# First pair of FFN up projections by eight plain products, token sums formed beside it, second norm at highest priority

## The chip, the cores and the metric

One core of a Trainium2 chip runs the whole program. The metric is the device time of one execution in microseconds (us), taken as the median of several runs. Engines are named as in the profile: PE is TensorE, DVE is VectorE, ACT is ScalarE, POOL is GpSimd, and SP is the queue from which most transfers are issued.

## What is computed

The reference is a two-layer trunk (a gated DeltaNet layer, then a retention layer). Each layer has a token mixer and a SwiGLU FFN. The change lies in the up projections of the first layer's FFN:

```python
x = x + gt1 * y                                   # end of the mixer
h = modulate(x, norm2_g[i], sh2, sc2)             # RMSNorm, scale, shift
x = x + gt2 * ((silu(h @ w1) * (h @ w3)) @ w2)    # the same for the context tokens
```

There are 512 latent and 256 context tokens, 1024 channels, and an FFN width of 2816, which is 22 tiles of 128 columns. All of it is in float32.

## The kernel before

A float32 operand is split into a high part that PE takes (fp32r) and a low remainder: ACT writes the high part (L113), DVE the low one (L114). A product is then three matmuls: high by high, low by high, high by low (`mm3`). The 768 tokens are joined in one tile `xj` (8 channel tiles by 768 tokens) and cut into two halves of 384, U1 and U2.

**The up projections** (`up_pairs`) take the 22 column tiles as 11 pairs. For one pair the work is a 2 by 2 block product: two column tiles, two halves of the channels, two halves of the tokens. Instead of eight block products the kernel forms seven, after Strassen and Winograd. The token blocks are `b11`, `b21` (U1, first and second channel half) and `b12`, `b22` (U2); the sums of them that the seven products need are `t1` to `t4`, made in `token_sums` on DVE (L447) with their high parts on ACT (L450). The weight sums `s1`, `s2` and two differences are made on POOL (L134). One block product is 24 matmuls of 128x384 (both of w1 and w3, four channel tiles, three matmuls each), so a pair is 168 matmuls.

**The first norm** (U1) is finished while the mixer's output projection still runs. Then `up_pairs` begins. Its first block product (`b11` by tile 0) needs only U1; `first` makes it and copies it to `p1`, and `second` adds the `b21` product and gates it. **The second norm** (U2) is a chain: POOL's last additions into `accj` (squares), the column sums on PE (`rstd_cols`, L315), about a dozen small operations on DVE (`rsqrt`, L169 to L176), three `diag` tiles spread by PE (L329), eight multiplications on DVE (L433), eight scalings on ACT (L440). Only then can `token_sums` begin, and five of the seven products of every pair need what it makes (`t1` to `t4`) or `b22` (`rest`). The kernel before opens pairs 0 and 1 (`first`, `second` of each), and after the token sums ends both with `rest`.

**The order** on each engine is made by the tile scheduler, which takes instructions by the place where they are written, or earlier where `high_priority()` stands around them; each engine then runs its instructions strictly in that order. DVE work marked with `keep_in_program_order` stays in the written order. The banks `psg` are three, and the converted weights are kept in rings of pools `wra`, `wrb` of two each. A raw weight tile is 1 MB, loaded by `up_load` from the SP queue: even tiles to pool `r8a`, odd ones to `r8b` and `r8c`. `xj` is given back after the token sums (`xjes.close()`); the pools opened behind it take its place. From pair 2 on `ada_rows` runs beside the products: every 10 groups of three matmuls it puts one load and one DVE reduction (L216 `prod`) into the stream, for the modulation of the next layer.

Of the kernel before, what the change touches and what calls it, by code (L numbers as in the profile page):

```python
# [10 lines left out]
F32 = mybir.dt.float32  # L11
# [18 lines left out]
J = 2  # L30
HALF = NT // 2
# [23 lines left out]
class Trunk:  # L55
# [370 lines left out]
    def norm_half(self, unit, r):  # L426
# [4 lines left out]
        for k in range(KT):  # L431
            x = self.xj[:, k, a:b]
            nc.vector.tensor_tensor(out=x, in0=x, in1=rb, op=ALU.mult)  # L433
            for st, lo, hi in PIECES[unit]:
# [4 lines left out]
                else:  # L439
                    nc.scalar.activation(out=v, in_=v, func=AF.Identity, scale=sc, bias=sh)  # L440

    def token_sums(self, pool):

        x, nc = self.xpart, self.nc

        def tt(o, a, b, op=ALU.subtract):
            self.tc.keep_in_program_order(nc.vector.tensor_tensor(out=o, in0=a, in1=b, op=op))  # L447

        at = lambda n, q, c: self.blocks[n][c][:, 2 * q:2 * q + 2, :]
        high = lambda n, q, src: nc.scalar.activation(out=at(n, q, 0), in_=src, func=AF.Copy)  # L450
        low = lambda n, q, src: tt(at(n, q, 1), src, at(n, q, 0).bitcast(F32))
        b11, b21, b12, b22 = ([x(h, u, q) for q in range(2)] for h in range(2) for u in range(2))
        for q in range(2):
            t3 = pool.tile([128, 2, HALF], F32, tag="t3", name="t3")
            tt(t3, b22[q], b12[q])
            tt(b11[q], t3, b11[q], ALU.add)
            high("t2", q, b11[q])
            high("t3", q, t3)
            tt(b21[q], b21[q], t3)
            low("t2", q, b11[q])  # L460
            low("t3", q, t3)
        for q in range(2):
            tt(b12[q], b22[q], b11[q])
            high("t1", q, b12[q])
        for q in range(2):
            low("t1", q, b12[q])
            high("t4", q, b21[q])
        for q in range(2):
            low("t4", q, b21[q])
            high("22", q, b22[q])  # L470
        for q in range(2):
            low("22", q, b22[q])

    def up_open(self, es):

# [11 lines left out]
        return new("") if kind == "s" else (new("h"), new("l"))  # L487

    def up_load(self, f):
        self.raws[f] = (self.ups["r"][0] if f % 2 == 0 else self.ups["r"][1:][f // 2 % len(self.ups["r"][1:])]).tile([128, 2, 1024], F32, tag="r", name="raw")  # L490
        self.nc.sync.dma_start(out=self.raws[f], in_=self.a["w13"][0, f].rearrange("j p c -> p j c"))

    def up_conv(self, src):
# [12 lines left out]
    def up_pairs(self, es, held):  # L506
# [3 lines left out]
        tt = nc.vector.tensor_tensor  # L510
        add, sub = ALU.add, ALU.subtract
        raws, blocks, conv = self.raws, self.blocks, self.up_conv
        self.block(self.pool(es, "late"), "t2", "t3", "t1", "t4", "22")
        pp = self.pool(es, "p1", 2)
        self.ups["w"].append(self.pool(es, "wrb", 2))
        self.ups["r"].append(self.pool(es, "r8c"))
        self.up_load(3)

        def product(ps, w, name, more=False):
            bh, bl = blocks[name]  # L520
# [18 lines left out]
        def first(w):  # L539
            a = bank()  # L540
            product(a, w, "11")
            p1 = pp.tile([128, 2, HALF], F32, name="p1")
            nc.scalar.activation(out=p1, in_=two(a), func=AF.Copy)
            return a, p1

        def second(i, a, w):
            product(a, w, "21", True)
            gate(a[:, 0, 0:HALF], a[:, 1, 0:HALF], 2 * i, U1)
# [25 lines left out]
            tt(out=u2, in0=two(c), in1=u2, op=add)  # L574
            gate(u2[:, 0, :], u2[:, 1, :], 2 * i, U2)

        a0, p0 = first(held["w"][0])
        w = conv(left(1)), conv(right(1))
        r = self.rstd_cols(U2, self.acc[J][:, U2[1]:U2[2]])
        a1, p1 = first(w[0])  # L580
        for q in range(2):
            tt(out=self.xpart(0, 1, q), in0=self.xpart(0, 1, q), in1=self.xpart(0, 0, q), op=sub)
        w2 = conv(held["sums"][1])
        self.norm_half(U2, r)
        second(0, a0, held["w"][1])
        second(1, a1, w[1])
        with ExitStack() as ts:
            self.token_sums(self.pool(ts, "tt"))
        self.xjes.close()
        begun = (a0, p0), (a1, p1)  # L590
        self.ups["s"].append(self.pool(es, "sb", 2))
        up = self.pool(es, "upk")
        ar = self.pool(es, "ar")
        for i in range(PAIRS):
            if i == 2:
                self.side, self.every = self.ada_rows(ar, ADA[0]), 10
            if i > 1:
                self.up_load(2 * i)
            if i > 1:
                self.up_load(2 * i + 1)  # L600
            if i < 2:
                rest(i, *begun[i], *((held["sums"], w2) if i == 0 else ()))
            else:
                a, p1 = first(conv(left(i)))
                rest(i, a, p1, mid=lambda: second(i, a, conv(right(i))))

    def down_groups(self, es, after):
        nc = self.nc
# [215 lines left out]
    def conv(self, pb, t):  # L824
        nc, cw = self.nc, self.cw
        cb = self.new([128, 770], "cb")
        nc.scalar.activation(out=cb, in_=pb[:, 0:770], func=AF.Copy, scale=cw[:, t, 0:1])  # L827
        for j in range(1, 5):
            last = nc.vector.scalar_tensor_tensor(out=cb, in0=pb[:, j:j + 770], scalar=cw[:, t, j:j + 1], in1=cb,  # L829
                                                  op0=ALU.mult, op1=ALU.add)  # L830
        return cb, last.ins
# [367 lines left out]
    def gdn(self):  # L1199
        nc, tc = self.nc, self.tc  # L1200
        with ExitStack() as es:
# [132 lines left out]
            for u in (U1, U2):  # L1334
                for m in range(KT):
# [14 lines left out]
                            for q in range(2):  # L1350
                                self.keep(name, q, self.xpart(0, up, q))
                    self.add_j(u, m, ps)
            held["sums"] = self.up_sums(0)
        return held

    def add_j(self, unit, m, ps):
# [301 lines left out]
```

## Time and profile before

| | |
|---|---|
| median of 3 runs | 2234.32 us (2232.72 to 2236.94) |
| profiled execution, own time | 2232.13 us |
| span of it in the trace | 2229.1 us |
| busy: PE, DVE, ACT, POOL | 2115.5, 1433.2, 835.5, 272.7 us |
| mean granted TensorE clock | 0.982 of full |

The profile page gives busy time per engine, the span in 40 slices, the chain of work that ended last, and the costliest groups of instructions. The trace answers narrower questions: a table of busy times by stretch (with the TensorE clock that was granted, as a share of full), a timeline by engine (start, duration, line, output and inputs, and in square brackets the idle time before it and what ended it), and the list of waits. A timeline row with "x2" stands for two instructions in a row. In the chain of waits 62% of the span is PE's products at L129.

### The profile page before, as it was taken

The numbers are of one execution on the slowest core, as the hardware profiler recorded it, in microseconds if no ns is written. First come the engines' busy times: TensorE is split into PE (matmuls) and PEld (weight loads), VectorE is DVE, ScalarE is ACT, GpSimd is POOL, SyncE is SP. The second block draws the span as 40 slices with busy tenths as digits, with TensorE's granted clock in tenths as the row PEclk, the third lists the DMA queues.
The fourth block names the chain that finished last, engine by engine and source line by source line (L and its number), as shares of the span: only waits on it lengthen the run. The fifth ranks groups of instructions, "written<-read, shape, count | busy, mean of one in ns | idle before, by whom it ended". The sixth has DMA issues, their size and how long they took to land.

```text
span 2229.1 us, 34569 instructions
## 1 busy us (share of the span) xinstructions
PE 2115.5 (95%) x13974; PEld 1825.6 (82%) x13974; DVE 1433.2 (64%) x2800; ACT 835.5 (37%) x1462; POOL 272.7 (12%) x218
## 2 busy tenths in 40 slices
PE   5899999999999779999999999999999999999997
PEld 2777887788767779999999988888888888888887
DVE  5786778677845768989766774645544466433435
ACT  3655656565623443333231242322222235222222
POOL 1322102221100533433100000000000000000000
PEclk9999999999999889999999999999999999999999
DMA  6221111111255333444475630312212123323221
GB/s 240 69 57 40 41 48 49 36 40 50 79 200 165 122 104 118 148 152 151 137 259 193 203 128 19 112 54 81 85 52 81 34 69 102 114 85 95 92 71 64
DMA packets 112384, 225.08 MB, mean 101 GB/s; under 512 B 47008, under 2 KB 60320, under 8 KB 111968
## 3 DMA queue, kind: packets, MB, share of 16 engines
q1 hardware_dynamic: 101264, 193.46, 26.7%
q10 hardware_dynamic: 8784, 23.07, 3.2%
q0 software_dynamic: 2176, 6.34, 0.9%
q8 instruction: 109, 1.79, 0.3%
q14 instruction: 51, 0.42, 0.1%
HBM read 203.84 MB, written 19.01 MB: 100 GB/s over the span
## 4 chain that ended last, share of the span: by engine, by line
PE 76%; DVE 10%; DMA 4%; ACT 4%; issue 3%; POOL 1%; SPq 0%; DVEq 0%; ACTq 0%; POOLq 0%
PE psg L129 62%; PE psx L129 13%; DVE wl L114 1%; DMA raw<-ada_t 1%; DVE cb L829 1%; PE psx L137 1%; DVE prod L216 1%; ACT wh L113 1%; DVE rsq_y L176 1%; DVE raw L216 1%; DMA graw<-gd 1%; ACT vd L1002 0%; DVE rsq_b L174 0%; DVE rsq_b L175 0%; DMA raw<-w 0%
## 5 line engine op out<-in xcount | busy, mean ns | idle before, releaser
L129 PE MATMUL psg<-hh,wh 128*128 128x512 f32 (+1 forms) x1152 | 426.3, 370 | 7.9 <-ACT pb L820 6.8
L129 PE MATMUL psg<-hl,wh 128*128 128x512 f32 (+1 forms) x1152 | 420.2, 365 | 2.0 <-POOL hl L284 1.7
L129 PE MATMUL psg<-hh,wl 128*128 128x512 f32 (+1 forms) x1152 | 418.9, 364 | 0.0
L113 ACT ACTIVATE wh<-raw 128x1024 fp32r<-128x1024 f32 (+1 forms) x203 | 209.0, 1030 | 553.9 <-PE psg L129 419.8
L114 DVE TENSOR_TENSOR wl<-raw,wh 128x1024 fp32r<-128x1024 f32 (+1 forms) x203 | 252.1, 1242 | 103.2 <-ACT wh L113 99.6
L129 PEld LDWEIGHTS psg<-hh,wh 128*128 128x128 f32 x1152 | 217.4, 189 | 38.8 <-ACT pb L820 8.0
L129 PEld LDWEIGHTS psg<-hl,wh 128*128 128x128 f32 x1152 | 217.6, 189 | 32.6 <-POOL hl L284 2.1
L129 PEld LDWEIGHTS psg<-hh,wl 128*128 128x128 f32 x1152 | 217.4, 189 | 30.3 <-DVE wl L114 0.2
L129 PE MATMUL psg<-gl,w2h 128*128 128x384 f32 (+2 forms) x560 | 193.4, 346 | 2.8 <-DVE gl L114 2.8
L129 PE MATMUL psg<-gh,w2h 128*128 128x384 f32 (+2 forms) x560 | 191.2, 346 | 4.4 <-ACT w2h L113 4.1
L129 PE MATMUL psg<-gh,w2l 128*128 128x384 f32 (+2 forms) x560 | 192.7, 345 | 0.4 <-DVE w2l L114 0.4
L354 DVE SCALAR_TENSOR_TENSOR x<-psg,mod,x 128x256 f32<-128x256 f32 (+3 forms) x192 | 105.1, 569 | 104.2 <-PE psg L129 103.7
L129 PEld LDWEIGHTS psg<-gh,w2h 128*128 128x128 f32 x560 | 105.8, 189 | 11.6 <-ACT w2h L113 4.4
L129 PEld LDWEIGHTS psg<-gl,w2h 128*128 128x128 f32 x560 | 106.3, 190 | 10.2 <-DVE gl L114 4.5
L129 PEld LDWEIGHTS psg<-gh,w2l 128*128 128x128 f32 x560 | 106.4, 190 | 6.5 <-DVE w2l L114 1.0
L829 DVE SCALAR_TENSOR_TENSOR cb<-pb,k_conv_w,cb 128x770 f32<-128x770 f32 x96 | 103.6, 1079 | 7.0 <-ACT cb L827 5.6
L216 DVE CUSTOM_DVE_ANT_0 raw<-raw,crow,k_ada_b 128x1024 f32<-128x1024 f32 x54 | 78.4, 1452 | 35.2 <-DMA raw<-ada_t 33.4
L113 ACT ACTIVATE w2h<-raw 128x1024 fp32r<-128x1024 f32 x48 | 50.5, 1056 | 113.8 <-PE psg L129 61.2
L129 PE MATMUL psg<-y,wh 128*128 128x512 f32 (+1 forms) x320 | 83.2, 350 | 0.0
L129 PE MATMUL psg<-wl,hh 128*128 128x512 f32 x192 | 75.0, 391 | 0.8 <-DVE wl L114 0.8
L129 PE MATMUL psg<-wh,hh 128*128 128x512 f32 x192 | 74.9, 390 | 0.0
L129 PE MATMUL psg<-wh,hl 128*128 128x512 f32 x192 | 74.9, 390 | 0.0
(406 smaller groups left out, 4451.5 us busy)
## 6 DMA issues: line engine op xcount, KB each, us to landing
raw<-w SPq DMA_DIRECT2D x88, 512.0 KB, 4.1
raw<-w_ret SPq DMA_DIRECT2D x64, 512.0 KB, 3.5
raw<-ada_t SPq DMA_DIRECT2D x54, 512.0 KB, 3.5
raw<-w SPq DMA_DIRECT2D x22, 1024.0 KB, 5.4
raw<-ada_w SPq DMA_DIRECT2D x42, 512.0 KB, 4.9
raw<-w_gdn ACTq DMA_DIRECT2D x31, 512.0 KB, 3.5
gd<-g SPq DMA_DIRECT2D x44, 192.0 KB, 1.8
graw<-gd SPq DMA_DIRECT2D x22, 384.0 KB, 4.7
```

Of the source, the lines that this page charges most:

```text
L113: nc.scalar.activation(out=hi, in_=src, func=AF.Copy)
L114: nc.vector.tensor_tensor(out=lo, in0=src, in1=hi.bitcast(F32), op=ALU.subtract)
L129: ins = self.nc.tensor.matmul(*args, **kw)
L137: ins = self.nc.tensor.transpose(out, in_, ident)
L176: nc.vector.scalar_tensor_tensor(out=y, in0=b, scalar=1.5, in1=y, op0=ALU.add, op1=ALU.mult)
L216: nc.vector.tensor_tensor_reduce(out=out, in0=raw, in1=cb[:, v, :], scale=1.0, scalar=self.adab[:, layer, col:col + 1], op0=ALU.mult, op1= ...
L354: self.nc.vector.scalar_tensor_tensor(out=x, in0=ps, scalar=self.mod[layer][:, 24 * which + 16 + m, 1 - st:2 - st], in1=x if src is None e ...
L829: last = nc.vector.scalar_tensor_tensor(out=cb, in0=pb[:, j:j + 770], scalar=cw[:, t, j:j + 1], in1=cb, op0=ALU.mult, op1=ALU.add)
```

## The change

Pair 0 (column tiles 0 and 1) is now formed by the plain eight products: `b11` and `b21` for both tiles, then, as soon as the second norm is ready, `b12` and `b22` for both. `b12` becomes a kept block of its own. Pair 1 is opened between the two (`first`, `second`). Its `rest`, and pairs 2 to 10, go on with seven products. The token sums, the weight sums of pair 1 and the splitting of `t1`, `t4` stand beside the eight products. The column sums, the whole second norm and the splitting of `b12` and `b22` stand in `high_priority()`. Tile 3 is loaded into the place of tile 1, a third ring of weights `wrc` is open meanwhile, and POOL's sums for pair 0 go.

```diff
+    def keep_block(self, name, src):
+        for q in range(2):
+            self.keep(name, q, src[q])
...
     def token_sums(self, pool):
...
         for q in range(2):
             tt(b12[q], b22[q], b11[q])
-            high("t1", q, b12[q])
-        for q in range(2):
-            low("t1", q, b12[q])
-            high("t4", q, b21[q])
-        for q in range(2):
-            low("t4", q, b21[q])
-            high("22", q, b22[q])
-        for q in range(2):
-            low("22", q, b22[q])
+        return b12, b21
...
-        self.raws[f] = (self.ups["r"][0] if f % 2 == 0 else self.ups["r"][1:][f // 2 % len(self.ups["r"][1:])]).tile([128, 2, 1024], F32, tag="r", name="raw")
+        self.raws[f] = (self.ups["r"][0] if f % 2 == 0 else self.ups["r"][1:][(f // 2 + 1) % len(self.ups["r"][1:])]).tile([128, 2, 1024], F32, tag="r", name="raw")
...
-        self.block(self.pool(es, "late"), "t2", "t3", "t1", "t4", "22")
+        self.block(self.pool(es, "late"), "t2", "t3", "22")
         pp = self.pool(es, "p1", 2)
         self.ups["w"].append(self.pool(es, "wrb", 2))
-        self.ups["r"].append(self.pool(es, "r8c"))
-        self.up_load(3)
...
-        a0, p0 = first(held["w"][0])
-        w = conv(left(1)), conv(right(1))
-        r = self.rstd_cols(U2, self.acc[J][:, U2[1]:U2[2]])
-        a1, p1 = first(w[0])
-        for q in range(2):
-            tt(out=self.xpart(0, 1, q), in0=self.xpart(0, 1, q), in1=self.xpart(0, 0, q), op=sub)
-        w2 = conv(held["sums"][1])
-        self.norm_half(U2, r)
-        second(0, a0, held["w"][1])
-        second(1, a1, w[1])
+        whole = lambda a, w, c: (product(a, w[0], "1" + c), product(a, w[1], "2" + c, True))
         with ExitStack() as ts:
-            self.token_sums(self.pool(ts, "tt"))
+            self.ups["w"].append(self.pool(ts, "wrc", 2))
+            self.block(self.pool(ts, "b12"), "12")
+            wa = [held["w"], [conv(raws[1][:, :, c:c + 512]) for c in (0, 512)]]
+            wb = conv(left(1)), conv(right(1))
+            self.up_load(3)
+            a = bank()
+            product(a, wa[0][0], "11")
+            with self.tc.high_priority():
+                r = self.rstd_cols(U2, self.acc[J][:, U2[1]:U2[2]])
+            product(a, wa[0][1], "21", True)
+            gate(a[:, 0, 0:HALF], a[:, 1, 0:HALF], 0, U1)
+            b = bank()
+            product(b, wa[1][0], "11")
+            with self.tc.high_priority():
+                for q in range(2):
+                    tt(out=self.xpart(0, 1, q), in0=self.xpart(0, 1, q), in1=self.xpart(0, 0, q), op=sub)
+                self.norm_half(U2, r)
+                for n, up in (("12", 0), ("22", 1)):
+                    self.keep_block(n, [self.xpart(1, up, q) for q in range(2)])
+            product(b, wa[1][1], "21", True)
+            gate(b[:, 0, 0:HALF], b[:, 1, 0:HALF], 1, U1)
+            begun = first(wb[0])
+            second(1, begun[0], wb[1])
+            t1, t4 = self.token_sums(self.pool(ts, "tt"))
+            sums = self.up_sums(1)
+            for f in range(2):
+                a = bank()
+                whole(a, wa[f], "2")
+                gate(a[:, 0, 0:HALF], a[:, 1, 0:HALF], f, U2)
+        self.ups["w"].pop()
+        self.nup["w"] = 0
+        w2 = conv(sums[1])
+        self.block(self.pool(es, "t14"), "t1", "t4")
+        self.keep_block("t1", t1)
+        self.keep_block("t4", t4)
         self.xjes.close()
-        begun = (a0, p0), (a1, p1)
+        self.ups["r"].append(self.pool(es, "r8c"))
...
-        for i in range(PAIRS):
-            if i == 2:
-                self.side, self.every = self.ada_rows(ar, ADA[0]), 10
...
+        rest(1, *begun, sums, w2)
+        self.side, self.every = self.ada_rows(ar, ADA[0]), 10
+        for i in range(2, PAIRS):
+            self.up_load(2 * i)
+            self.up_load(2 * i + 1)
+            a, p1 = first(conv(left(i)))
+            rest(i, a, p1, mid=lambda: second(i, a, conv(right(i))))
...
-            held["sums"] = self.up_sums(0)
```

What this makes of the order on the engines is shown at three places. The first is PE at the very start of the up projections; `accj` holds the sums of squares of the second norm, `psx` of L315 their column sums, `b11h`, `b11l` and `b21h` are parts of the first half's blocks.

```order
@@ -2934,4 +2934,5 @@
 L129 MATMUL psg<-b11h,wl 128x384
 L129 MATMUL psg<-b11h,wh 128x384
+L315 MATMUL psx<-ones,accj 128x2 x3
 L129 MATMUL psg<-b11l,wh 128x384
 L129 MATMUL psg<-b11h,wl 128x384
@@ -2954,5 +2955,30 @@
 L129 MATMUL psg<-b11l,wh 128x384
 L129 MATMUL psg<-b11h,wl 128x384
-L315 MATMUL psx<-ones,accj 128x2 x3
+L129 MATMUL psg<-b21h,wh 128x384
```

The column sums stood behind all 24 matmuls of the first block product; now they stand behind the fourth.

The second place is DVE at the same time. L1361 (L1374 in the changed code) takes the last two pieces of the mixer's output out of PSUM, L582 (L588) is the subtraction of `b11` from `b21` that the token sums need, L318 begins the second norm's small chain. In the kernel before:

```order
L114 TENSOR_TENSOR b21l<-xj,b21h 128x768 x2
L1361 SCALAR_TENSOR_TENSOR xj<-psx,mod_76,xp 128x384 x2
L114 TENSOR_TENSOR wl<-raw,wh 128x1024 x2
L582 TENSOR_TENSOR xj<-xj 128x2x384 x2
L318 TENSOR_SCALAR rms_s<-psx 128x3
```

and in the changed one:

```order
L114 TENSOR_TENSOR b21l<-xj,b21h 128x768 x2
L588 TENSOR_TENSOR xj<-xj 128x2x384 x2
L1374 SCALAR_TENSOR_TENSOR xj<-psx,mod_76,xp 128x384 x2
L114 TENSOR_TENSOR wl<-raw,wh 128x1024 x2
L318 TENSOR_SCALAR rms_s<-psx 128x3
L169 TENSOR_SCALAR rsq_y<-rms_s 128x3
L114 TENSOR_TENSOR wl<-raw,wh 128x1024
```

The two subtractions moved ahead of the last two evictions, and two conversions of weights moved in among the small operations.

The third place is DVE behind the second norm's multiplications (L433). In the kernel before the gates `g` of the first products and two conversions stand between them and the token sums (L447):

```order
L433 TENSOR_TENSOR xj<-xj,psx 128x384 x8
L114 TENSOR_TENSOR wl<-s,wh 128x1024
L536 TENSOR_TENSOR g<-g,psg 128x384
L114 TENSOR_TENSOR wl<-raw,wh 128x1024
L536 TENSOR_TENSOR g<-g,psg 128x384
L447 TENSOR_TENSOR t_9026<-xj 128x768
```

and in the changed one (token sums are L451, gates L530):

```order
L433 TENSOR_TENSOR xj<-xj,psx 128x384 x8
L114 TENSOR_TENSOR b12l<-xj,b12h 128x768 x2
L114 TENSOR_TENSOR b22l<-xj,b22h 128x768 x2
L530 TENSOR_TENSOR g<-g,psg 128x384 x3
L451 TENSOR_TENSOR t_9086<-xj 128x768
L451 TENSOR_TENSOR xj<-t_9086,xj 128x2x384
L451 TENSOR_TENSOR xj<-xj,t_9086 128x2x384
L451 TENSOR_TENSOR bt2l<-xj,bt2h 128x768
```

The low parts of `b12` and `b22` come first now, then three gates in a row, the third of which belongs to pair 1's second product, and the token sums stand behind it.

## Rows read from the trace of the kernel before

**Rows 1.** Table by stretch (us): busy time and count by engine, granted clock.

```profile
760.00:780.00 20.00, 13.25 (x69) 12.90 (x69) 14.05 (x25) 6.22 (x9) 12.78 (x6) 0.81 0.01 2
780.00:800.00 20.00, 12.61 (x51) 10.99 (x50) 16.97 (x20) 13.08 (x18) 0.00 (x0) 0.70 0.21 72
800.00:820.00 20.00, 13.88 (x66) 13.28 (x65) 12.55 (x12) 5.39 (x5) 15.51 (x6) 0.84 0.39 132
...
1000.00:1050.00 50.00, 49.84 (x285) 49.23 (x284) 46.54 (x47) 16.50 (x20) 19.12 (x8) 1.00 0.43 149
```

**Rows 2.** Timeline of PE, 740 to 850 us: start, duration, instruction, idle before it.

```profile
756.65 0.66 PE L129 MATMUL psg<-b11h,wh 128*128 128x384 f32 x1 [6.17 <-ACT sq L1366]
...
759.67 0.53 PE L129 MATMUL psg<-b11h,wh 128*128 128x384 f32 x1
759.99 0.53 PE L129 MATMUL psg<-b11l,wh 128*128 128x384 f32 x1
...
762.83 0.73 PE L315 MATMUL psx<-ones,accj 128*128 128x2 f32 x6
...
774.58 1.22 PE L329 MATMUL psx<-diag,ones 128*128 128x128 f32 x4 [6.75 <-DVE diag L328]
...
790.40 0.69 PE L129 MATMUL psg<-bt2h,wh 128*128 128x384 f32 x1 [5.01 <-ACT bt2h L450]
...
795.13 0.69 PE L129 MATMUL psg<-bt2h,wh 128*128 128x384 f32 x1 [1.76 <-ACT bt2h L450]
...
816.63 0.69 PE L129 MATMUL psg<-bt4h,wh 128*128 128x384 f32 x1 [6.12 <-DVE u L565]
...
848.88 0.33 PE L129 MATMUL psg<-b11h,wh 128*128 128x384 f32 x1
```

**Rows 3.** Chain of waits, in order of time: two pieces of it in the later pairs.

```profile
1010.83 42.37 PE psg L129 x240
...
1055.91 3.35 DVE prod L216
```

**Rows 4.** Timeline of DVE, 755 to 800 us.

```profile
755.37 1.13 DVE L1361 SCALAR_TENSOR_TENSOR xj<-psx,mod,xp 128x384 f32<-128x384 f32 x2
756.43 2.35 DVE L114 TENSOR_TENSOR wl<-raw,wh 128x1024 fp32r<-128x1024 f32 x2
758.70 1.82 DVE L582 TENSOR_TENSOR xj<-xj 128x768 f32<-128x768 f32 x2
...
765.06 2.25 DVE L174 SCALAR_TENSOR_TENSOR rsq_b<-rsq_y 128x3 f32<-128x3 f32 x1
...
773.06 0.16 DVE L174 SCALAR_TENSOR_TENSOR rsq_b<-rsq_y 128x3 f32<-128x3 f32 x1
773.26 0.16 DVE L175 TENSOR_TENSOR rsq_b<-rsq_b,rms_s 128x3 f32<-128x3 f32 x1
...
776.59 3.80 DVE L433 TENSOR_TENSOR xj<-xj,psx 128x384 f32<-128x384 f32 x8 [0.89 <-PE psx L329]
...
792.25 0.96 DVE L447 TENSOR_TENSOR t<-xj 128x768 f32<-128x768 f32 x1
...
796.85 1.82 DVE L447 TENSOR_TENSOR xj<-xj 128x768 f32<-128x768 f32 x2
```

**Rows 5.** Timeline of POOL, 756 to 773 us, and the sums `accj` as a group.

```profile
756.74 5.72 POOL L134 TENSOR_TENSOR accj<-accj,sq 128x384 f32<-128x384 f32 x2 [0.43 <-ACT sq L1366]
762.42 2.38 POOL L134 TENSOR_TENSOR s<-raw 128x1024 f32<-128x1024 f32 x1
764.88 2.41 POOL L134 TENSOR_TENSOR s<-s,raw 128x1024 f32<-128x1024 f32 x1
...
L134 POOL TENSOR_TENSOR accj<-accj,sq x14: 994/1020/4631, 726.5 to 761.5; 128x384 f32<-128x384 f32 x14
```

**Rows 6.** Timeline of ACT, 777 to 784 us.

```profile
777.18 4.91 ACT L440 ACTIVATE xj<-xj,mod,A 128x384 f32<-128x384 f32 x8 [6.45 <-DVE xj L433]
...
782.36 1.57 ACT L450 ACTIVATE b22h<-xj 128x768 fp32r<-128x768 f32 x2
```

**Rows 7.** Transfers issued from 735 to 860 us: count, KB, median us to landing.

```profile
raw<-w SPq DMA_DIRECT2D x5, 1024.0 KB, 5.2
```

**Rows 8.** Waits of PE, 750 to 1125 us: total, times, longest.

```profile
PE psg L129 <- DVE u L559: 2.4, 4, 0.8
```

More of the change, by code (lines that the diff above doesn't have):

```diff
@@ L440, in norm_half @@
                     nc.scalar.activation(out=v, in_=v, func=AF.Identity, scale=sc, bias=sh)
+    def keep_block(self, name, src):
+        for q in range(2):
+            self.keep(name, q, src[q])
     def token_sums(self, pool):
-        x, nc = self.xpart, self.nc
+        nc = self.nc
         def tt(o, a, b, op=ALU.subtract):
@@ L451, in token_sums @@
         low = lambda n, q, src: tt(at(n, q, 1), src, at(n, q, 0).bitcast(F32))
-        b11, b21, b12, b22 = ([x(h, u, q) for q in range(2)] for h in range(2) for u in range(2))
+        b11, b21, b12, b22 = ([self.xpart(h, u, q) for q in range(2)] for h in range(2) for u in range(2))
         for q in range(2):
@@ L593, in up_pairs @@
         ar = self.pool(es, "ar")
-        for i in range(PAIRS):
-            if i == 2:
-                self.side, self.every = self.ada_rows(ar, ADA[0]), 10
[L597 to L605, printed above, removed]
+        rest(1, *begun, sums, w2)
[5 more added lines that the diff above has]
+            rest(i, a, p1, mid=lambda: second(i, a, conv(right(i))))
     def down_groups(self, es, after):
```

## The prediction

> **What bounds the kernel now.** I read the slices of the page first: PE is busy in nine tenths or more nearly everywhere, so a change has to be read where it is not. The table by stretch shows that place: from 760 to 820 us PE is busy 13.25, 12.61 and 13.88 of each 20 us, at a granted clock of 0.81, 0.70 and 0.84 [rows 1]. PE's timeline says why: the wait for the second norm (6.75 us), for the token sums (5.01 and 1.76) and for the first pair's weight differences (6.12) [rows 2]. Behind each wait matmuls follow each other at 0.32 us (759.67 to 759.99), the lower of the two clocks, 1.2 GHz [rows 2]. In the later pairs 240 matmuls take 42.37 us, 0.177 us each, the higher clock [rows 3]. So this stage is bound by a chain through POOL, DVE and ACT, and everything around it by PE.
>
> The stage before, in one number: from its first matmul at 756.65 to the first of pair 2 at 848.88 are 92.2 us [rows 2]. In it stand two pairs, 336 matmuls. At 0.177 us they would take 59.5. **The stage loses 32.7 us** to waits and to the lower clock. The waits named are 6.75 + 5.01 + 1.76 + 6.12 = 19.6; the other 13 are mostly low clock.
>
> **The change, part by part.** I walk through the changed order with the durations of before, in before's time.
>
> *More matmuls.* Pair 0 takes 8 x 24 = 192 instead of 168: 24 x 0.177 = **+4.2 us**, on PE, with no cover. Pair 1 stays: 360 in all, 63.7 us.
>
> *The start.* The two subtractions go ahead of the last two evictions on DVE, and PE's first matmul waits for the second of these. They take 1.82 us [rows 4]: **PE starts 1.8 us later**, at 758.45.
>
> *The column sums now stand behind the fourth matmul,* so PE stops at 758.45 + 4 x 0.32 = 759.7 until POOL has closed `accj`; everything else of PE is queued behind. When is that? One addition takes 1.02 us in the median, but 4.63 at most: the first of the last two began at 756.74, while DVE ran operations with both inputs in SBUF until 760.5, and both were done at 762.4 [rows 4, 5]. Now DVE runs the subtractions, the evictions (one input from PSUM) until 758.3, and two conversions (2.35 us) until 760.6. Then two additions of 1.0: `accj` is closed at about 762.6. PE stands 2.9 us. Bounds: the additions may slip in ahead of the conversions (760.6, a wait of 0.9), or be held once more by the length of a conversion (763.8).
>
> *The small chain.* Before, the operations of L169 to L176 took 764 to 774, since single ones took 2.25 us while POOL formed weight sums, against 0.16 later [rows 4, 5]. Now POOL's first wide sum waits for tile 3, whose load waits for the conversions of tile 1; that load (5.2 us, [rows 7]) lands at about 772.5. So the chain runs undisturbed: from 763.6 a dozen operations at 0.2 us from start to start [rows 4], and the two conversions moved in among them (half of 2.35 each): 768.9. PE has the 20 + 4 matmuls ahead of `diag`; from 763.5, some ten of them at 0.32 (the lower clock held for over 3 us behind 756.65, [rows 2]) and the rest at 0.177, they end at 769.1. The wait of 6.75 us is gone. The `diag` matmuls cost 1.2 us [rows 2].
>
> *Second norm to `b12`, `b22`.* DVE multiplies from 770.6 (3.80, [rows 4]); ACT scales 4.91 from the first on [rows 6] until 776, then splits four blocks at 0.79 (1.57 for two, [rows 6]) until 779; DVE's low parts follow, then gate 0: about 781. PE meanwhile has 20 + 48 + 24 matmuls on U1 alone (16.2 us with the `diag` of 1.2 before them): until 786. `b12` is ready 5 us before it is wanted. This is the cover that the eight products buy.
>
> *The token sums* stand behind the third gate, which needs pair 1's `second`. PE ends that at 791.2 (six `b12` matmuls are put in ahead of it, which hide the copy `p1`). DVE from there: silu and gate 1.2 us; two rounds of token sums at 4.6 each (792.25 to 796.85, [rows 4]); two more sums 1.82, two conversions 2.35, three low parts and two gates, one more low part, a third conversion: 792.4 + 9.2 + 1.8 + 2.35 + 4 x 0.91 + 2 x 0.55 + 1.2 = 811.7. PE has 18 + 24 + 48 matmuls of pair 0 and 24 of `t2`, 114 x 0.177 = 20.2, until 811.4, and then wants just that conversion (of `s1`, for `t1`). It fits within half a microsecond; I take **0.5 us** of waits here. The waits of 5.01 and 1.76 are gone. So is that of 6.12: tile 3 is here at 772.5 and POOL has the sums of pair 1 done by some 782, long before PE wants them at 807; POOL's sums of pair 0 (four of about 2.4 us) are not made at all.
>
> *Loads.* Tile 5's load now waits for the token sums' scratch and goes out near 804. It lands near 809, its sums take POOL until 815 to 818, and PE wants them at about 833: covered by 15 us. Even tiles load as before.
>
> *Later.* Pairs 2 to 10 keep their order but for the places where `prod` is put in, since the count of groups is shifted by eight. DVE is busy 46.5 of 50 us there [rows 1], and PE waits for L559 2.4 us in all [rows 8]. I take no change, with 2 us either way. Nothing behind the pairs changes its order.
>
> **The sum.** Losses of the stage now: between 758.45 and 769.1 pass 10.65 us for 28 matmuls worth 5.0, so 5.7; `diag` 1.2; waits 0.5; and 0.5 for the steps between banks: 7.9. Pair 2 begins at 758.45 + 63.7 + 7.9 = 830.0 instead of 848.9: **a gain of 18.9 us**. In parts: 32.7 lost before against 7.9 now is 24.8; less 4.2 of matmuls, less 1.8 of start.
>
> Against the profiled execution's own 2232.1 that gives 2213.2; against the median of the three runs, 2.2 higher, 2215.4. I say 2214.
>
> **A rule beside the rows.** DVE operations with two SBUF inputs and POOL's wide sums held each other up, 2.25 against 0.16 us and 4.63 against 1.02 [rows 4, 5]. The Trainium skill (SBUF — State Buffer, "Who interferes with whom") has the rule: such a DVE operation and a GpSimd operation that reads SBUF share a port under an exclusive lock, and the second to issue fully blocks. The trace agrees. By that rule the new place of POOL's sums is no accident without a price, and it makes rival B.
>
> **Rivals.**
>
> *B. POOL's sums of pair 1 fall on the low parts of `b12` and `b22`.* They run from 772.5 to 782, and DVE's four low parts from 777. If each of the four waits for one sum as L174 did (about 2.4 us), gate 0 comes at 781 + 9.6 = 790.6, and PE, which needs its bank for `b12` at 786, stands 4.6 us; with 1.5 to 3 us of lower clock behind it the gain is 11 to 13: 2220 to 2223. Against it: in the rows POOL lost whenever DVE's operations came back to back (4.63 us), and the four do.
>
> *C. The gain is eaten within the stage.* DVE's chain behind the third gate fits by nothing. If its operations are a fifth slower than in the rows, PE stands 4 us at `t1`, drops to the lower clock, and with B added the gain falls to about 4: 2230. Against it: POOL is idle there, so nothing is seen that would slow DVE.
>
> *D. Slower than before: `prod` in the nine later pairs.* DVE is nearly full there. The shifted count can put a pair of `prod` operations (3.35 us, [rows 3]) just ahead of the `u` sum (L559 or L565) that PE's next product needs. At up to 3.35 in each of nine pairs it costs up to 30 us, and the change ends slower from 18.9 + 4.5 = 23.4, or 2.6 us a pair, on; at the full price 2245. Against it: before, such collisions are there too, four waits of at most 0.8 us [rows 8], and the order in which `prod` stands among the `u` sums differs in few places.
>
> *E. It does not do what it says.* The high priority could leave the norm where it was. The order shows the contrary (the column sums 20 matmuls earlier), so this has no share of its own; what priority costs, the later start and the early stop of PE (1.8 + 2.9), is in the sum.
>
> **How the numbers follow.** Forecast 0.78, with the bounds 2208 (no stop at the column sums, 2 us less; no waits; 2 us from the later pairs) to 2219 (the column sums late by 1.2, 2 us more low clock). B 0.12, C 0.06, D 0.04. For 8 in 10 and a little more, on both sides: 2207 to 2224, which holds the forecast and B. A change under 0.2% (4.5 us) can't be told from none here. Faster by more: the forecast, B and a small part of C, 0.91; the same: most of C, 0.05; slower: D, 0.04.
>
> **What would show it.** Right: PE's first up matmul about 1.8 us later; a stop of 1 to 4 us ahead of L315; no wait above 1 us at `diag`, `b12`, `t2` or `t4`; the granted clock near 1.00 from 770 on; the first `b11` of pair 2 18 to 20 us earlier. Wrong: a wait of several us at the first `b12` (B), at `t1` (C), or waits at L553 or L559 of the changed code beyond 1 us in most later pairs (D); a clock that stays at its lower level between 770 and 800.

## The result and the profile after

The changed kernel takes 2219.35 us, the median of 4 runs (2217.68 to 2224.36), against 2234.7 for the kernel before (4 runs): a ratio of 0.9935, 95% interval 0.9916 to 0.9954. In a second set it took 2219.19 (5 runs, 2216.21 to 2222.29) against 2235.68 (21 runs): 0.9926, interval 0.9914 to 0.9939. That is a gain of 15.4 and 16.5 us. The forecast was 18.9 us and 2214. Direction, stage and mechanism were right; some 3 us that the stage won were lost again behind it, at two places that the prediction had set at nothing.

The profiled run after took 2220.4 us, its span 2218.6. The table by stretch, in the columns of [rows 1]:

```profile
760.00:780.00 20.00, 17.52 (x85) 16.78 (x86) 11.71 (x28) 9.03 (x14) 10.52 (x5) 0.77 0.21 74
780.00:800.00 20.00, 20.00 (x117) 19.82 (x116) 12.69 (x13) 5.86 (x9) 3.62 (x2) 1.00 0.08 30
800.00:820.00 20.00, 20.00 (x116) 19.94 (x115) 17.97 (x19) 11.41 (x14) 7.31 (x2) 1.00 0.46 159
```

Where PE was busy for 12.61 and 13.88 of 20 us it is now busy for all 20, at a granted clock of 1.00 instead of 0.70 and 0.84. PE's timeline shows what is left of the stops of [rows 2]:

```profile
759.84 0.66 PE L129 MATMUL psg<-b11h,wh 128*128 128x384 f32 x1 [7.91 <-ACT sq L1379]
...
763.94 1.44 PE L315 MATMUL psx<-ones,accj 128*128 128x2 f32 x6 [2.48 <-POOL accj L134]
...
771.30 0.60 PE L329 MATMUL psx<-diag,ones 128*128 128x128 f32 x4
...
772.06 0.49 PE L329 MATMUL psx<-diag,ones 128*128 128x128 f32 x2
...
830.22 0.33 PE L129 MATMUL psg<-b11h,wh 128*128 128x384 f32 x1
```

There is one stop, for `accj`; the `diag` matmuls and everything behind them start without a wait. From the first up matmul to the first `b11` of pair 2 (the last row) are 70.38 us, against 92.23 in [rows 2].

To compare kernels apart from what varies between executions, I cut each trace at matmuls that all of them have: **start** is from the last matmul of the stage before to the first up matmul; **stage** from there to pair 2; **pairs** from there to the last up matmul; **gap** from there to the first matmul of the down projections (on `w2h`).

```
us                                     start   stage   pairs     gap     sum
before                                  6.51   92.23  268.84    4.41  371.99
before, once more                       6.50   92.22  269.00    4.44  372.16
changed                                 8.24   70.38  270.58    5.95  355.15
changed, once more                      8.22   70.55  270.52    6.35  355.64
eight products, no priority             6.48   73.19  270.31    6.29  356.27
seven products, priority                6.48   95.83  268.99    4.43  375.73
changed, blocks in other order          8.24   70.23  270.72    4.55  353.74
changed, count of groups + 6            8.24   70.14  267.90    5.88  352.16
changed, last accj sums on DVE          8.71   70.61  270.50    6.18  356.00
changed, subtractions not first         6.48   73.07  270.40    6.22  356.17
... and three diag                      5.71   71.35  270.65    6.00  353.71
blocks + count                          8.23   70.48  267.28    4.59  350.58
blocks + count + subtr. + diag          5.74   71.25  267.14    4.40  348.53
blocks + count + diag, no priority      5.74   74.08  267.52    4.31  351.65
```

The same kernel gives the same four numbers within 0.2 us (0.4 for the gap). So the change is worth 372.1 - 355.4 = 16.7 us here, close to what the medians say (15.4 and 16.5): 20.0 won in start and stage, 1.6 lost in the pairs, 1.7 lost in the gap.

### The profile page after: what moved, and what is told of

Its sections match the earlier page's. It is cut to its first block, busy times and chain, and to the rows that moved or that the text cites. A ratio compares the mean times of both kernels' runs of the same rounds, so it can differ in the third digit from the quotient of the medians.

```text
span 2218.6 us, 34604 instructions
## 1 busy us (share of the span) xinstructions
PE 2115.2 (95%) x13998; PEld 1824.8 (82%) x13998; DVE 1424.7 (64%) x2794; ACT 831.7 (37%) x1460; POOL 264.3 (12%) x214
## 4 chain that ended last, share of the span: by engine, by line
PE 75%; DVE 10%; DMA 6%; ACT 3%; issue 3%; POOL 1%; SPq 0%; DVEq 0%; ACTq 0%; POOLq 0%
PE psg L129 60%; PE psx L129 13%; DMA raw<-ada_t 2%; DVE prod L216 1%; DVE wl L114 1%; DVE raw L216 1%; PE psx L137 1%; DVE cb L843 1%; DMA raw<-w 1%; DVE g L530 0%; DVE rsq_y L176 0%; ACT wh L113 0%; DMA dx<-dr 0%; DMA graw<-gd 0%; DVE rsq_b L174 0%
```

## The experiments

**The two kernels once more.** Both are unchanged; the question is what belongs to the change and what to the execution.

> The changed kernel once more, word for word. Theory T1 (the changed stage did what was worked out, and the 3 to 4 us that are missing from the gain of 18.9 are variation of other stages from one execution to the next): from the first up matmul to the first b11 of pair 2 again 70 to 71 us, against 92.2 before; outside that stage the places where it lost (the wait for w2h ahead of the down projections, 5.6 us; the slow clock of 0.84 at the start of the retention) differ from the first profile; the median gain lies anywhere between 13 and 19 us. Theory T2 (the change itself costs 3 to 8 us in the later pairs and behind them): the gain is 15 us again within 1.5, the wait for w2h is 5.6 again, and the clock at 1305 to 1325 us is 0.84 again.

> The kernel before once more, word for word. T1: stages whose instructions are alike in both kernels differ between two of its own profiles by 1 to 4 us (first column sum at 738.4, wait for w2h of 4.1, clock of 1.00 at the start of the retention in the first profile). T2: these three figures come again as they were, and the differences to the changed kernel are the change's.

The changed kernel took 2219.19 us again, the kernel before 2236.03 (ratio to the pooled 21 runs 1.0001, 0.9992 to 1.0009). Both theories were half right. Stage, pairs and gap came again, so the 3.3 us lost there are the change's (for T2). The rest was not: the last matmul of the stage before, where both kernels are alike, fell at 750.14 and 752.67 us in the two profiles of before and at 751.60 and 756.59 in those of after; from the first matmul on `w2h` to the end passed 1106.97 and 1111.37 before, 1111.85 and 1108.17 after. The slow clock at the start of the retention, which the first profile of the changed kernel has (granted clock 0.89 from 1300 to 1330 us), is not in its second one (1.00, as before): that was the execution's (for T1).

**Which half of the change does it?** One kernel keeps eight products and moved sums, without the priority:

```diff
-            with self.tc.high_priority():
-                r = self.rstd_cols(U2, self.acc[J][:, U2[1]:U2[2]])
+            r = self.rstd_cols(U2, self.acc[J][:, U2[1]:U2[2]])
...
-            with self.tc.high_priority():
-                for q in range(2):
...
```

> The eight products and the moved token sums stay, but the second norm has no priority: it is put among the conversions in the order of the code. The column sums then stand behind 24 matmuls of b11 and the two subtractions behind the evictions. By the walk of the prediction: PE starts 1.8 us earlier and does not stop 2.5 us for accj, but four conversions (2.35 us for two) and two subtractions (1.82) stand ahead of the norm's small operations, so b12 is ready near 789 while PE, with 96 matmuls that need U1 alone, wants it near 779: a wait of 8 to 10 us and 2 to 3 us of slow clock. Gain 9 to 12 us, some 6 to 8 us slower than the change. Rival: priority buys nothing here, since what it brings early it costs in the late start and the stop: then within 2 us of the change.

It took 2218.59 us (ratio to before 0.9923, interval 0.991 to 0.9937): no slower than the change by time, and 1.0 us slower by start and stage (79.67 against 78.62 and 78.77). The 8 to 10 us at `b12` did not come. PE's waits of this kernel, 730 to 1130 us (total, times, longest; one of the two waits for `accj`, 0.5 us, belongs to the first norm):

```profile
PE psx L329 <- DVE diag L328: 2.3, 2, 1.8
PE psx L315 <- POOL accj L134: 2.1, 2, 1.6
```

DVE's timeline at the first of them:

```profile
773.34 4.60 DVE L328 TENSOR_SCALAR diag<-k_ident,rsq_y 128x128 f32<-128x128 f32 x2
```

And POOL's:

```profile
757.90 7.97 POOL L134 TENSOR_TENSOR accj<-accj,sq 128x384 f32<-128x384 f32 x2 [0.44 <-ACT sq L1377]
768.20 2.40 POOL L134 TENSOR_TENSOR s<-raw 128x1024 f32<-128x1024 f32 x1 [2.33 <-DVE rsq_b L174]
```

My walk let PE run through to `b12` at 779, behind 96 matmuls. In fact 120 stand ahead of it, since pair 1's first product is among them (24, or 4.2 us). PE also stood 1.6 us at the column sums and 2.3 at `diag`, and some 28 matmuls followed each other at about 0.32 us, which is 4 us more than at the higher clock. So it asked for `b12` at 788.72 only, when it was there. The late norm cost a little at each of its own steps and nothing at the end of them. Note POOL's two additions, 7.97 us beside four conversions and two subtractions of DVE, and DVE's two `diag`, 4.60 us beside POOL's sums where the changed kernel takes 0.48.

The other kernel is the one before, with column sums and second norm at highest priority and nothing else:

```diff
-        r = self.rstd_cols(U2, self.acc[J][:, U2[1]:U2[2]])
+        with self.tc.high_priority():
+            r = self.rstd_cols(U2, self.acc[J][:, U2[1]:U2[2]])
...
-        self.norm_half(U2, r)
+        with self.tc.high_priority():
+            self.norm_half(U2, r)
```

> The kernel before with its seven products and its order of token sums, but column sums and second norm at highest priority. Walk: PE stops for accj behind 4 matmuls (about 3 us), has 24 fewer matmuls that need U1 alone ahead of the second norm, and the waits of 5.01 + 1.76 us for token sums and of 6.12 for the weight sums of pair 1 stay, since nothing moves these. Gain 0 to 5 us: without the eight products the priority has no cover. Rival: the priority alone brings most of the gain (over 9 us), and the eight products are only its price of 4.2 us.

2238.76 us, ratio 1.0016 (interval 1.0007 to 1.0025): 3 us slower, where I gave it 0 to 5 of gain. PE's waits from 730 to 850 us (total, times, longest):

```profile
PE psg L129 <- ACT bt2h L450: 7.2, 2, 5.4
...
PE psg L129 <- DVE u L565: 6.1, 1, 6.1
PE psx L329 <- DVE diag L328: 4.9, 1, 4.9
PE psx L315 <- POOL accj L134: 3.0, 2, 2.5
```

The stop at `accj` is new, the wait at `diag` fell only from the 6.75 us of [rows 2] to 4.9, the others stayed. Priority without cover is a loss here. The eight products with the moved sums, without any priority, bring 15.8 of the 16.7 us by the table (372.1 - 356.3). No run has the eight products without the moved sums, or the other way round, so how these two share the gain is not shown.

**The gap ahead of the down projections.** SyncE's queue says what changed there; first before, then after:

```profile
1111.82 4.48 SPq L537 DMA_DIRECT2D gd<-g  x2
1116.40 0.38 SPq L628 DMA_DIRECT2D graw<-gd  x1
1116.83 0.45 SPq L119 DMA_DIRECT2D raw<-w  x1
```

```profile
1094.96 4.50 SPq L531 DMA_DIRECT2D gd<-g  x2
1101.17 0.32 SPq L642 DMA_DIRECT2D graw<-gd  x1
1101.54 0.42 SPq L119 DMA_DIRECT2D raw<-w  x1
```

Before, the loads go out right behind the stores and 1.3 us ahead of the last up matmul (1117.72). After, the first of them waits until the last up matmul (1100.80) is through; the waits of SyncE's queue name it:

```profile
SPq L642 <- PE psg L129: 1.6, 1, 1.6
```

The built program's addresses give the reason. `graw` takes bytes 60672 to 63744 of each partition in both kernels. Before, `bt1h` lay over its first part (56576 to 62720); with `t1` and `t4` moved to a pool of their own, `b22h` lies there, which the very last product reads. The experiment puts another block there:

```diff
-        self.block(self.pool(es, "late"), "t2", "t3", "22")
+        self.block(self.pool(es, "late"), "t2", "22", "t3")
```

> The changed kernel, but for the order of three blocks in one pool: t2, 22, t3 instead of t2, t3, 22. Theory: the 1.7 us that the changed kernel loses ahead of the down projections (5.95 and 6.35 us from the last up matmul to the first with w2h, 4.4 before) come from memory: the first load of graw lies at 60672 to 63744 bytes, over block 22 (56576 to 62720) that the very last product reads, where before it lay over t1. With block 22 moved away the load goes out ahead of the last product: gap 4.4 us again, time 1.7 us shorter, stage (78.7 from the last matmul of the stage before to pair 2) and pairs (270.6) as they were. Rival: the gap comes from the queue of stores or from a slower transfer, and stays 6 us.

2217.35 us (0.9918, 0.9903 to 0.9933); gap 4.55 us. SyncE's queue in this kernel, where the last up matmul starts at 1102.03:

```profile
1096.19 4.50 SPq L531 DMA_DIRECT2D gd<-g  x2
1100.79 0.38 SPq L642 DMA_DIRECT2D graw<-gd  x1
1101.23 0.45 SPq L119 DMA_DIRECT2D raw<-w  x1
```

The theory stands: a wait on memory, 1.4 to 1.8 us, with no instruction out of its order.

**The pairs.** Four of nine pairs take 30.6 to 31.2 us in the changed kernel, three before (30.6 to 31.3); the others 29.2 to 29.9. DVE's timeline ahead of such a pair's first `u` sum:

```profile
868.57 1.27 DVE L216 CUSTOM_DVE_ANT_0 prod<-raw,crow,k_ada_b 128x1024 bf16<-128x1024 f32 x1
...
869.78 1.22 DVE L114 TENSOR_TENSOR wl<-s,wh 128x1024 fp32r<-128x1024 f32 x1
870.91 1.27 DVE L216 CUSTOM_DVE_ANT_0 raw<-raw,crow,k_ada_b 128x1024 f32<-128x1024 f32 x1
...
872.12 0.95 DVE L553 TENSOR_TENSOR u<-psg,p 128x768 f32<-128x768 f32 x1
```

The two modulation rows stand about the conversion, and PE waits 0.73 us for the `u` sum (873.12). Which pairs end so is set by the count of groups, which the eight products moved by eight. One line moves it on:

```diff
+        self.ticks += 6
         self.side, self.every = self.ada_rows(ar, ADA[0]), 10
```

> The changed kernel with the count of groups moved on by 6, so that the modulation rows (prod, L216) fall elsewhere among the u sums of pairs 2 to 10. Theory: a pair takes 30.6 us instead of 29.3 when prod, the conversion of s1 and the second prod stand in this order just ahead of its first u sum; in the changed kernel that is so at four pairs, before at three, here at two. Pairs 2 to 10: 270.6 becomes 267.9 (two long pairs fewer, 1.35 each), below the 268.9 of before; stage and gap unchanged; time 2.7 us shorter. Rival: the long pairs come from loads or from the bank of PSUM and stay at four: 270.6.

2213.72 us (0.9907, 0.9888 to 0.9926), the pairs 267.90, as worked out. By its median this kernel gains 22.2 us on the kernel before, by the table 19.9; four runs can't tell these apart. PE's waits for `u` from 740 to 1130 us fall with it, first after, then here:

```profile
PE psg L129 <- DVE u L553: 3.1, 5, 0.7
```

```profile
PE psg L129 <- DVE u L553: 2.0, 4, 0.7
```

So rival D's mechanism was there. With some 1.35 us for a pair that it meets (0.7 of it the wait) and one such pair more than before, it cost 1.6 us, 0.2 a pair over all nine, where 2.6 a pair would have decided. That the count sets which pairs are long is shown; no run puts it back to just where it stood before, so that it makes up all of the 1.6 us is likely but not shown.

**The stop at the column sums.** Its row after, in POOL's timeline:

```profile
759.93 3.96 POOL L134 TENSOR_TENSOR accj<-accj,sq 128x384 f32<-128x384 f32 x2 [0.44 <-ACT sq L1379]
```

And DVE beside it:

```profile
759.62 2.35 DVE L114 TENSOR_TENSOR wl<-raw,wh 128x1024 fp32r<-128x1024 f32 x2
```

The two additions end 1.9 us behind the conversions (763.89 and 761.97), as if the first had waited for them; alone, one takes 1.02 [rows 5]. The experiment forms the last three on DVE:

```diff
-            self.pool_tt(out=acc, in0=acc, in1=sq, op=ALU.add)
+            if unit == U2 and m > 4:
+                self.tc.keep_in_program_order(nc.vector.tensor_tensor(out=acc, in0=acc, in1=sq, op=ALU.add))
+            else:
+                self.pool_tt(out=acc, in0=acc, in1=sq, op=ALU.add)
```

> The changed kernel with the last three additions to accj (second unit) on DVE instead of POOL. Theory: the stop of 2.5 us ahead of the column sums is POOL held off accj by DVE's operations with both inputs in SBUF (two additions of 1.02 us took 3.96 here). On DVE an addition of 128 x 384 takes about 0.55, so accj is closed by 761 to 762 in the first profile's time, the column sums (now behind 9 matmuls) wait less than 0.3, and the stage from the last matmul before it to pair 2 takes 75.5 to 77.5 us instead of 78.7, with 0.5 to 1.1 lost at the start to additions that stand ahead of the evictions. Rival: accj is late because ACT's squares are late; then the wait stays above 1.5.

The stop went, as the theory has it, and the time stayed: 2219.41 us (0.993, 0.9908 to 0.9952), start and stage 79.3. The 2.5 us turned up elsewhere: 0.5 in the start, 1.8 as a wait one step later, and the rest in more matmuls at the lower clock (20 instead of 13 followed at 0.32 us). DVE's timeline in this kernel:

```profile
771.28 2.08 DVE L328 TENSOR_SCALAR diag<-k_ident,rsq_y 128x128 f32<-128x128 f32 x1 [2.92 <-PE psx L329]
```

POOL's:

```profile
770.93 2.34 POOL L134 TENSOR_TENSOR s<-raw 128x1024 f32<-128x1024 f32 x1 [22.84 <-DMA raw<-w]
```

PE's wait for it:

```profile
PE psx L329 <- DVE diag L328: 1.8, 1, 1.8
```

The third `diag` had met POOL's first weight sum.

**The start.** The same happens when the two subtractions are taken from ahead of the evictions:

```diff
             with self.tc.high_priority():
-                for q in range(2):
-                    tt(out=self.xpart(0, 1, q), in0=self.xpart(0, 1, q), in1=self.xpart(0, 0, q), op=sub)
                 self.norm_half(U2, r)
...
+            for q in range(2):
+                tt(out=self.xpart(0, 1, q), in0=self.xpart(0, 1, q), in1=self.xpart(0, 0, q), op=sub)
             product(b, wa[1][1], "21", True)
```

> The changed kernel with the two subtractions (L588, 1.82 us) taken out of the priority; they then stand among the small operations of the norm and no longer ahead of the last two evictions. Theory: the first up matmul comes 1.7 us earlier (6.5 us behind the last matmul before it, not 8.2), and the subtractions take the same 1.8 us out of the norm's chain, which has a cover of 1.5 to 2 us at diag and more at b12: stage 77.0 to 78.2 us instead of 78.7. Rival: the chain to b12 has no cover left and the stage stays 78.7 or becomes longer.

PE starts 1.76 us earlier and the stage is 2.7 longer: 2218.22 us (0.9917, 0.9897 to 0.9937), by the table 0.9 slower in start and stage, against my theory. PE waits 1.74 us at `diag`. DVE's row there, and POOL's:

```profile
776.83 2.05 DVE L328 TENSOR_SCALAR diag<-k_ident,rsq_y 128x128 f32<-128x128 f32 x1 [2.47 <-PE psx L329]
```

```profile
776.46 2.35 POOL L134 TENSOR_TENSOR s<-raw 128x1024 f32<-128x1024 f32 x1 [9.96 <-DMA raw<-w]
```

With two buffers the third `diag` waits until PE has read the first. It comes 0.4 us behind the start of POOL's first weight sum and then takes 2.05 us. In the changed kernel it slipped in ahead, 1.1 us before POOL began:

```profile
771.72 0.29 DVE L328 TENSOR_SCALAR diag<-k_ident,rsq_y 128x128 f32<-128x128 f32 x1 [1.44 <-PE psx L329]
```

```profile
773.13 2.41 POOL L134 TENSOR_TENSOR s<-raw 128x1024 f32<-128x1024 f32 x1 [9.24 <-DMA raw<-w]
```

A third buffer takes that wait away:

```diff
-            dg = self.small.tile([128, 128], F32, tag="diag", name="diag", bufs=2)
+            dg = self.small.tile([128, 128], F32, tag="diag", name="diag", bufs=3)
```

> The kernel with the two subtractions out of the priority, and with three buffers for diag instead of two. Theory: in the kernel with two buffers the third diag had to wait for PE to read the first, fell into POOL's first weight sum and took 2.05 us instead of 0.29, so PE stood 1.74 us; written 0.2 us behind the other two it is done before POOL begins. No wait at diag, and the stage from the last matmul before it to pair 2 takes 76.5 to 77.7 us instead of 79.6. Rival: the small chain as a whole is too late for PE, and the wait only moves to the first diag: 79 us or more.

2213.33 us (0.991, 0.9891 to 0.993), start and stage 77.06, no wait at `diag`. The group of the three, from 755 to 790 us:

```profile
L328 DVE TENSOR_SCALAR diag<-k_ident,rsq_y x3: 280/281/286, 768.0 to 768.4; 128x128 f32<-128x128 f32 x3
```

Of the 2.5 us won, 1.7 is the wait; the other 0.77 is in the start (6.48 to 5.71), where the third buffer moves the first norm's `diag` too: its third one stands right behind the second now, and behind an eviction without it.

**All together.** Three kernels join the edits: blocks and count; these with subtractions and diag; and blocks, count and diag without any priority.

> The changed kernel with both later losses undone: blocks in the order t2, 22, t3 and the count of groups moved on by 6. Theory: the two are independent and add up: gap 4.5 us, pairs 2 to 10 in 267.9, stage 78.5 as in the changed kernel; 4.3 us shorter than the changed kernel, a gain of 20 to 21 us on the kernel before. Rival: an earlier start of the down projections only meets later loads of w2, and half of it is lost there: a gain of 18.

> Both later losses undone, the subtractions out of the priority and three buffers for diag. Theory: stage 76.5 to 77.7, pairs 267.9, gap 4.5: 1 to 2 us less than with the two undone alone, a gain of 21 to 23 us on the kernel before. Rival: the stage is bound elsewhere (the slow clock behind the first matmuls), and this is within 0.5 us of the kernel with the two undone alone.

> Both later losses undone and three buffers for diag, but no priority for the second norm at all (order of the code). Theory: without priority the stage took 79.7 us, with waits of 1.6 (column sums) and 2.3 (diag, held by POOL's weight sums); the third buffer takes away at most half of the second, since POOL's sums began at 768.2 there and the small chain ran until 773: stage 78 to 79.5, 1 to 2 us behind the version with priority for the norm alone. Rival: priority is worth nothing: within 0.5 us of it.

They took 2212.63 (0.9909, 0.9891 to 0.9927), 2212.29 (0.9904, 0.9886 to 0.9922) and 2211.08 us (0.9902, 0.9882 to 0.9922). The runs can't tell the three apart; by the ratios all beat the kernel before by about 20 to 22 us, and these ratios lie 0.0017 to 0.0024 (4 to 5 us) below the second one of the changed kernel, though the intervals still overlap (0.9914 to 0.9939). The traces can: the sums of the table are 350.58, 348.53 and 351.65, against 355.4 for the change. The two later losses add up as expected (4.8 us); the better start brings 2 more; and in this one profile without priority 3 of them go. The expected cause, a rest of the wait at `diag`, did not come: PE has no wait there, but 1.1 us at `b12l` and this one (740 to 1130 us):

```profile
PE psg L129 <- DVE wl L114: 4.3, 1, 4.3
```

DVE's timeline at that place, and POOL's:

```profile
808.15 3.33 DVE L114 TENSOR_TENSOR wl<-raw,wh 128x1024 fp32r<-128x1024 f32 x1
811.41 3.35 DVE L114 TENSOR_TENSOR wl<-s,wh 128x1024 fp32r<-128x1024 f32 x1
```

```profile
808.00 2.40 POOL L134 TENSOR_TENSOR s<-raw 128x1024 f32<-128x1024 f32 x1 [22.85 <-DVE bt4l L114]
810.48 3.20 POOL L134 TENSOR_TENSOR s<-s,raw 128x1024 f32<-128x1024 f32 x1
```

This is the place of rival C, the conversion of `s1` that `t1` wants. Its row is 3.35 instead of 1.22 us, because POOL's sums of pair 2 have come to lie on it. Whether that falls so in every execution of this kernel, one profile can't say; by the median it is the fastest of the three.

## Why the prediction was right, and where its size was off

The range held, the direction and the place too. Step by step:

- *The start, 1.8 us later:* 8.24 - 6.51 = 1.73. Right.
- *The stop for `accj`, 2.9 us:* 2.48, by the mechanism named (POOL held until the two conversions end, at 761.97 where 760.6 was forecast for a start 1.4 us earlier).
- *The small chain undisturbed, 5.3 us from column sums to norm:* the rows stand from 765.42 to 770.28, 4.9 us. Right. (The prediction's own terms, twelve operations at 0.2 and 2.35, add up to 4.75 and not 5.3; PE was the later of the two in its walk, so nothing hung on it.) It rests on POOL's sums, which began 2.9 us behind the chain and 1.1 behind the third `diag`: where an experiment moved the chain or the sums, the third `diag` was hit.
- *The losses of the stage, 7.9 us:* 70.38 - 63.7 = 6.7, from two errors that partly cancel. Up to the first `diag` 28 matmuls stood as walked, and with the stop among them they took 11.46 us instead of 10.65: 0.8 more. From there 332 matmuls took 58.92 us, 0.2 above 0.177 each, where 2.2 was forecast. The 0.177, taken from a long piece of later pairs, already held the steps between banks, and the 0.5 us at `t1` did not come.
- *`b12` ready 5 us before it is wanted:* rival B's mechanism did come. DVE's low parts:

```profile
778.86 5.58 DVE L114 TENSOR_TENSOR b12l<-xj,b12h 128x768 fp32r<-128x768 f32 x2 [2.46 <-ACT b12h L113]
784.36 1.81 DVE L114 TENSOR_TENSOR b22l<-xj,b22h 128x768 fp32r<-128x768 f32 x2
```

  and POOL's sums beside them:

```profile
778.12 2.42 POOL L134 TENSOR_TENSOR raw<-raw 128x1024 f32<-128x1024 f32 x1
780.51 3.12 POOL L134 TENSOR_TENSOR raw<-raw,s 128x1024 f32<-128x1024 f32 x1
```

  It cost 3.8 us (5.58 - 1.81) instead of 9.6. The first part waited for POOL's third sum, which ended at 780.54; POOL's last sum, held in its turn, took 3.12 us instead of 2.4 and held the second part until 783.62; then POOL had none left, and the other two parts ran alone. So the prediction's reason against B, that POOL loses to four operations in a row, did not hold; that only two sums were left did it. The cover of 5 us was counted to gate 0, which frees the bank of the first `b12` product:

```profile
786.10 1.00 DVE L530 TENSOR_TENSOR g<-g,psg 128x384 f32<-128x384 f32 x2
```

```profile
788.20 0.33 PE L129 MATMUL psg<-b12h,wh 128*128 128x384 f32 x1
```

  Gate 0, the first of the two, ends at 786.6, so 1.6 us of the 5 were left. The cover held, with little to spare.
- *The fit at `t1` (rival C):* it held by 0.24 us, and in part by order. The prediction's reason against C, that POOL is idle there, does not agree with its own walk of POOL's sums of tile 5, and the rows have both at once:

```profile
812.30 1.21 DVE L114 TENSOR_TENSOR wl<-s,wh 128x1024 fp32r<-128x1024 f32 x1
```

```profile
812.61 4.31 POOL L134 TENSOR_TENSOR s<-raw 128x1024 f32<-128x1024 f32 x1 [28.99 <-DVE bt4l L114]
```

  DVE's conversion began 0.3 us ahead, ended at 813.52, and PE took it at 813.76; it was POOL that waited. In the last of the joined kernels, without priority, POOL came first, and PE stood 4.3 us. So far start and stage: 20.0 us won, where 18.9 was forecast.
- *Pairs 2 to 10, "I take no change, with 2 us either way":* this term was off in size: -1.6 us, within its bounds, and the run with the count moved on shows that the count sets the length of these pairs. Rival D's price was misread: the 3.35 us of [rows 3] are one `prod` operation beside POOL's sum, not a pair (DVE's row there is 1055.82, 3.43 us, and the second one follows with 3.30).
- *"Nothing behind the pairs changes its order":* true of the order, and not enough: the place in memory of a block moved, and the first load behind the pairs waited for it, 1.7 us. This term was missing. I had followed queues and buffers of the pairs, not what the next stage's tiles would lie upon.

18.9 + 1.1 - 1.6 - 1.7 = 16.7 us. The rest of the distance to 2214 is the level: the prediction stood on runs of before with a median of 2234.3, and 21 later ones gave 2235.7; 2235.7 - 16.7 = 2219.0, against 2219.2 and 2219.35 measured.

## What to carry to other kernels

When a chain is the bound, first give PE work that doesn't need it: here eight products and sums moved beside them won 19 us of the stage without any priority, for 24 matmuls more. Priority for the chain alone lost 3 us; beside the eight products it brought 1 us, or 3 once the later losses were mended, by the table alone: the medians show neither. When blocks move between pools, look up what the next stage's first loads lie upon: a load that lands on what the last product reads waits for it, and no order of instructions shows that. When a count that places side work shifts, check which operations it now stands ahead of; one constant was worth 2.7 us by the table.

## What the runs showed that was not expected

The hold between DVE's operations with two inputs in SBUF and POOL's wide sums was known from [rows 4, 5]. Not expected was that it also catches an operation with one tensor and a column of scalars: a `diag` of 0.29 us took 2.05 and 2.08 when it began 0.35 to 0.4 us behind a sum of POOL, and 0.29 when it began ahead. The Trainium skill (SBUF — State Buffer, "Who interferes with whom") names `tensor_scalar` among the operations that can take the port pair shared with GpSimd, and says that the issue order decides who blocks; the rows of `diag` agree. POOL's addition of 759.93 does not fit so simply: the second of the two conversions began behind it (760.75), and POOL waited for that one too. Taking away that stop of 2.5 us gained nothing, since most of it came back where the work behind it met POOL's sums.

Two executions of one kernel put the same instructions up to 5 us apart by 750 us, and yet repeat a stage's own length within 0.2 us. Differences of 1 to 3 us, which medians of 4 to 6 runs can't tell, can be read from the lengths of stages in single profiles, if the stage is cut at the same two matmuls; how well that repeats rests on two kernels profiled twice.
